# Token-major gates and branches, keys split around the mixer's output product, and PSUM as three pairs and two banks

## The chip, the cores and the metric

One core of one Trainium2 chip runs the whole program; the other cores are idle. The metric is the device time of one execution in microseconds. A core has TensorE (PE, with its weight loads listed as PEld), VectorE (DVE), ScalarE (ACT), GpSimd (POOL) and SyncE (SP, whose queue issues the weight DMAs). Each executes its own instructions in order and waits on semaphores for the others. PE writes its results to PSUM, whose eight banks of 128x512 float32 are read back by DVE and ACT.

## The reference

Two layers over 256 tokens of width 1024, in float32:

```python
for l in range(DEPTH):
    x = x + 0.5 * swiglu(rms_norm(x, ffn1_norm[l]), ffn1_w_gu[l], ffn1_w_down[l])
    h = rms_norm(x, mix_norm[l])
    z = h @ w_in[l]
    q_a, k_a, v_a, q_b, f_b, i_b, og_b, gate_a, gate_b = jnp.split(z, split_at, axis=-1)
    # rotary on q_a, k_a; dilated_attention over 3 groups x 4 heads; y_a (T, 1024):
    y_a = dilated_attention(q_a, k_a, v_a) @ w_att_branch[l]       # 512 -> 1024
    # gated linear recurrence over 8 heads, norm per head:
    o_b = rms_norm(hgrn2_recurrence(q_b, f_b, i_b, lb_all[l]), hgrn_head_norm[l])
    o_b = o_b * jax.nn.silu(og_b)
    y_b = o_b @ w_hgrn_branch[l]                                   # 1024 -> 1024
    merged = jax.nn.sigmoid(gate_a) * y_a + jax.nn.sigmoid(gate_b) * y_b
    x = x + merged @ w_mix_out[l]
    x = x + cross_attention(rms_norm(x, xattn_norm[l]), rms_norm(mem, mem_norm[l]), ...)
    x = x + 0.5 * swiglu(rms_norm(x, ffn2_norm[l]), ffn2_w_gu[l], ffn2_w_down[l])
return rms_norm(x, final_norm)
```

The output gate `og_b` and the two mixer gates are 1024 wide each. Cross-attention has 4 heads of 256 and takes its keys and values from 256 memory tokens, which do not depend on `x`.

## The kernel before, in words

**Products.** Every product is done in split form: a float32 operand is cast to a high part (fp32r) and the rest is kept as a low part, and three of the four partial products are summed. The weights stream from memory in chunks of 16 blocks of 128x128, in the order in which the program takes them. ACT casts half a chunk (8 blocks, called a half here) to its high part (`whi`, L104), DVE subtracts it for the low part (`wlo`, L110). High parts are made three halves ahead of use and low parts two (`prep`, called by `take`, L113). Five buffers hold high parts, four hold low parts.

There are two loops. The feature-major loop `fm` (L303) has the weight block stationary and the activation moving: one matmul of 512 columns (high and low part of the 256 tokens, L316) and one of 256 (L317) a block; its result has features on partitions and tokens along the row. ACT copies one half out of PSUM (L337) and DVE adds the other (L340). The token-major loop `tm` (L347) has 128 tokens of the activation stationary and four weight blocks moving (512 columns): three matmuls (L290 to L292) for each of two token tiles, six for four blocks. Its result has tokens on partitions and is complete in PSUM. Before the change `tm` is used for the values of both mixers (L809, L819) and of cross-attention.

**Order.** The program's order is written out by the code as it runs; nothing reorders it. At the first `take` of each half, `tick` (L179) runs deferred evacuations that are due and then one step of a side job: the recurrence `hgrn` (L610) and the attention heads (L712) are generators that yield between steps, and take turns. In most of the mixer a step is taken every second half (`pace`). `drain` (L760) runs what is left at the end of the mixer's input products. A norm runs the same way with precedence (`urgent_norm`, L405).

**PSUM.** One pool of four pairs (two banks each). `pair()` is what `fm` and `tm` accumulate in; `bank()` (L153) takes a whole pair and uses half of it. The recurrence's step that computes its output holds two (L674) until the norm's scale is applied to them in its next step (L693).

**The mixer.** `mixer` (L767) runs 8 feature-major products for the recurrence's forget gates and queries, then 12 for attention queries and keys (`query_key`), between them the values and the output gate (`out_gate`, L835: 4 feature-major products) and 3 of the 8 mixer gate products (`gate`, L869); 5 more gate products follow. The gates are multiplied by the norm's scale on DVE (L830), and ACT applies Silu (L838) and Sigmoid (L872) to whole tiles of 128x1024. The recurrence's output is transposed by PE to feature-major (L702), multiplied there by gain and output gate on DVE (L707) and split into high and low part. The branches (L890 to L901) are 8 feature-major products, each with 4 attention blocks and 8 recurrence blocks for one 128-wide column of the result; DVE multiplies by the gates (L896), adds (L898), and ACT and DVE split the sum. Then comes the output product `w_mix_out` (`mm_resid`, L903).

**Cross-attention.** `xattn` (L940) begins with four feature-major products for keys, then four for queries, whose heads' scores are side jobs; values are token-major; at the end four heads write one bank each (12 matmuls of 256 columns, L286 to L288), which ACT casts (L270) and DVE subtracts (L273).

## Time and profile before

| | |
|---|---|
| runs | 1644.33, 1646.98, 1646.46 us; median 1646.46 |
| profiled execution | 1643.66 us, of which the span is 1641.9 us |
| PE, PEld, DVE, ACT, POOL busy | 1624.8, 1415.7, 1236.6, 926.1, 65.6 us |
| mean granted PE clock | 0.998 |
| weights | 288.94 MB moved in all, mean 176 GB/s; a chunk of 1 MB lands in 4.8 us |
| layer 0: first feed-forward, mixer's input products, branches, output product, cross-attention, second feed-forward | to about 196 us, 477, 510, 534, 638, 822 |

The page's first part gives busy time of each engine; a busy engine may still wait inside an instruction, and PE's rows overlap. The chain of waits follows the end back to what released it. The answers by time list each instruction with its start, its duration, the engine, the line and the tiles, and in brackets how long the engine was idle just before and which instruction ended that. A view by stretch gives, between two times, the busy time of each engine and the number of instructions that touch the stretch. Rows "x6" are six like instructions in a row, with one duration from the first's start to the last's end.

### The profile page before, as it was taken

The numbers are of one execution on the slowest core, as the hardware profiler recorded it, in microseconds if no ns is written. First come the engines' busy times: TensorE is split into PE (matmuls) and PEld (weight loads), VectorE is DVE, ScalarE is ACT, GpSimd is POOL, SyncE is SP. The second block draws the span as 40 slices with busy tenths as digits, with TensorE's granted clock in tenths as the row PEclk, the third lists the DMA queues.
The fourth block names the chain that finished last, engine by engine and source line by source line (L and its number), as shares of the span: only waits on it lengthen the run. The fifth ranks groups of instructions, "written<-read, shape, count | busy, mean of one in ns | idle before, by whom it ended". The sixth has DMA issues, their size and how long they took to land.

```text
span 1641.9 us, 26458 instructions
## 1 busy us (share of the span) xinstructions
PE 1624.8 (99%) x10818; PEld 1415.7 (86%) x10818; DVE 1236.6 (75%) x1808; ACT 926.1 (56%) x1385; POOL 65.6 (4%) x46
## 2 busy tenths in 40 slices
PE   9999999999999999999999999999999999999998
PEld 7888888888888888888888888888888888888887
DVE  7887696767868868877677777967678788688764
ACT  6665445566655656655456555445565656466542
POOL 0000000111100000000000000010110000000000
PEclk9999999999999999999999999999999999999999
DMA  8455444444445534555455564444444445355552
GB/s 305 180 191 211 189 155 173 162 157 152 154 150 184 183 151 167 193 188 197 183 185 196 182 224 177 162 155 160 174 142 159 162 179 181 129 206 180 194 189 79
DMA packets 41593, 288.94 MB, mean 176 GB/s; under 512 B 4864, under 2 KB 4992, under 8 KB 7424
## 3 DMA queue, kind: packets, MB, share of 16 engines
q1 hardware_dynamic: 41040, 286.67, 48.7%
q8 instruction: 85, 1.39, 0.3%
q10 hardware_dynamic: 432, 0.59, 0.1%
q14 instruction: 36, 0.29, 0.1%
HBM read 286.18 MB, written 1.05 MB: 175 GB/s over the span
## 4 chain that ended last, share of the span: by engine, by line
PE 86%; DVE 9%; ACT 2%; issue 2%; POOL 0%; DMA 0%; POOLq 0%; ACTq 0%
PE pair L316 46%; PE pair L317 23%; DVE wlo L110 3%; PE pair L290 3%; PE pair L292 3%; PE pair L291 3%; DVE join L340 1%; PE pair L636 1%; DVE join L896 1%; PE pair L720 1%; PE pair L754 1%; PE pair L329 1%; DVE slot L273 0%; PE pair L288 0%; PE pair L287 0%
## 5 line engine op out<-in xcount | busy, mean ns | idle before, releaser
L316 PE MATMUL pair<-slot,whi 128*128 128x512 f32 x3808 | 1342.0, 396 | 2.8 <-DVE slot L273 2.5
L317 PE MATMUL pair<-slot,wlo 128*128 128x256 f32 x3808 | 1066.1, 280 | 0.0
L316 PEld LDWEIGHTS pair<-slot,whi 128*128 128x128 f32 x3808 | 713.7, 187 | 165.8 <-ACT whi L104 3.1
L317 PEld LDWEIGHTS pair<-slot,wlo 128*128 128x128 f32 x3808 | 719.2, 189 | 0.8
L110 DVE TENSOR_TENSOR wlo<-raw,whi 128x1024 fp32r<-128x1024 f32 x532 | 641.6, 1221 | 40.6 <-ACT whi L104 40.3
L104 ACT CAST whi<-raw 128x1024 fp32r<-128x1024 f32 x532 | 546.8, 1047 | 16.6 <-issue 8.5
L337 ACT COPY join<-pair 128x512 f32<-128x512 f32 x136 | 79.4, 585 | 181.9 <-PE pair L317 181.8
L340 DVE TENSOR_TENSOR join<-pair,join 128x512 f32<-128x512 f32 x136 | 93.7, 690 | 99.9 <-ACT join L337 99.7
L280 ACT ACTIVATE slot<-x,vecs 128x256 fp32r<-128x256 f32 x64 | 30.8, 505 | 134.0 <-DVE x L427 132.8
L290 PE MATMUL pair<-whi,slot 128*128 128x512 f32 x224 | 89.7, 401 | 0.0
L292 PE MATMUL pair<-whi,slot 128*128 128x512 f32 x224 | 87.5, 391 | 0.0
L291 PE MATMUL pair<-wlo,slot 128*128 128x512 f32 x224 | 87.4, 390 | 0.0
L427 DVE SCALAR_TENSOR_TENSOR x<-pair,x 128x256 f32<-128x256 f32 (+1 forms) x80 | 42.4, 530 | 50.3 <-PE pair L317 48.8
L270 ACT CAST slot<-join 128x256 fp32r<-128x256 f32 (+1 forms) x120 | 51.7, 435 | 50.2 <-DVE join L898 26.0
L337 ACT COPY slot<-pair 128x512 f32<-128x512 f32 x48 | 28.0, 583 | 68.6 <-PE pair L317 68.6
L504 ACT ACTIVATE tmp<-join 128x256 f32<-128x256 f32 x88 | 36.4, 418 | 53.2 <-DVE join L503 53.2
L503 DVE TENSOR_TENSOR join<-join,bc 128x512 f32<-128x512 f32 x88 | 60.5, 693 | 5.1 <-ACT bc L403 2.4
L340 DVE TENSOR_TENSOR slot<-pair,slot 128x512 f32<-128x512 f32 x48 | 33.0, 688 | 35.6 <-ACT slot L337 35.6
L856 POOL TENSOR_TENSOR join<-join,sinb 128x512 f32<-128x512 f32 x24 | 44.7, 1860 | 378.0 <-ACT join L855 366.2
L273 DVE TENSOR_TENSOR slot<-join,slot 128x256 fp32r<-128x256 f32 (+1 forms) x120 | 54.0, 455 | 2.8 <-ACT slot L270 2.8
L292 PEld LDWEIGHTS pair<-whi,slot 128*128 128x128 f32 x224 | 42.1, 188 | 9.2
L281 DVE SCALAR_TENSOR_TENSOR slot<-x,vecs,slot 128x256 fp32r<-128x256 f32 x64 | 29.6, 483 | 27.0 <-ACT slot L280 27.0
(184 smaller groups left out, 1027.7 us busy)
## 6 DMA issues: line engine op xcount, KB each, us to landing
raw<-w SPq DMA_DIRECT2D x266, 1024.0 KB, 4.8
slot<-mem SPq DMA_DIRECT2D x6, 512.0 KB, 6.6
raw<-w SPq DMA_DIRECT2D x3, 512.0 KB, 7.5
y<-slot SPq DMA_DIRECT2D x3, 256.0 KB, 2.3
cst<-cst SPq DMA_DIRECT2D x1, 721.0 KB, 10.2
x<-x SPq DMA_DIRECT2D x2, 256.0 KB, 4.2
x<-x SPq DMA_DIRECT2D x1, 512.0 KB, 6.8
raw<-w SPq DMA_DIRECT2D x1, 256.0 KB, 4.4
```

Source lines behind the costliest of these rows:

```text
L104: nc.scalar.copy(self.hi[i], r)
L110: nc.vector.tensor_tensor(self.lo[i], r, self.hi[i].bitcast(F32), op=OP.subtract)
L270: nc.scalar.copy(h, src)
L273: nc.vector.tensor_tensor(l, src, h.bitcast(F32), op=OP.subtract)
L290: nc.tensor.matmul(out, ah, wh, start=first, stop=False)
L291: nc.tensor.matmul(out, ah, wl, start=False, stop=False)
L292: nc.tensor.matmul(out, al, wh, start=False, stop=last)
L316: nc.tensor.matmul(whole[:, i * 512:(i + 1) * 512], wh, act.parts(k), start=k == 0, stop=False)
L317: nc.tensor.matmul(whole[:, i * 512:i * 512 + T], wl, act.hi(k), start=False, stop=k == K - 1)
L337: nc.scalar.copy(d, right)
L340: nc.vector.tensor_tensor(d, left, d, op=OP.add)
L503: nc.vector.tensor_tensor(two(t), two(t), both(n.bc), op=OP.mult)
```

## The change

1. PSUM becomes three pairs and a second pool of two single banks, which `bank()` now takes from. The recurrence's two output banks become one pair; the final norm's statistics take a pair.
2. The output gate and the mixer gates become token-major: 2 products of 512 columns instead of 4, and 4 instead of 8. ACT copies them out of PSUM with the norm's scale. The recurrence's output is multiplied by the output gate before it is transposed (one step more), and the gain goes into the split after it.
3. The branches become token-major, attention first and recurrence second, for two halves of 512 columns. DVE multiplies by the gates and adds; then PE turns the sum back to feature-major, four blocks of 128 columns in two banks, two calls of `tick` later, and ACT and DVE split it.
4. Half of the cross-attention keys (two of the four products) move ahead of the output product of the mixer.
5. The order of the input products is written anew. A side job steps at every half from the tenth query-key product on, as before.

```diff
-    psum = ent(tc.tile_pool(name="psum", bufs=4, space=bass.MemoryType.PSUM))
+    psum = ent(tc.tile_pool(name="psum", bufs=3, space=bass.MemoryType.PSUM))
+    psum1 = ent(tc.tile_pool(name="psum1", bufs=2, space=bass.MemoryType.PSUM))
...
     def bank():
-        return pair()[:, :512]
+        return psum1.tile([P, 512], F32, name="bank")
...
-    def tm(name, l, c, act, evac):
+    def tm(name, l, c, act, evac, K=KD):
...
-        bs = [bank(), bank()]
+        both_tiles = pair()
+        bs = [both_tiles[:, :512], both_tiles[:, 512:]]
...
         while ("og", l) not in flags:
             yield True
+        for i in range(2):
+            o = os_[:, 512 * i:512 * (i + 1)]
+            nc.vector.tensor_tensor(o, o, sog[i][:, hh * 512:(hh + 1) * 512], op=OP.mult)
+        yield
         for i in range(2):
             b = bank()
...
-            for h in range(2):
-                k = 4 * hh + 2 * i + h
-                o = tmp()
-                nc.vector.scalar_tensor_tensor(o, b[:, h * T:(h + 1) * T], vec("hgrn_head_norm", l, k),
-                                               sog(k), op0=OP.mult, op1=OP.mult)
-                out.put(k, o, later=1)
+            for f in (out.high_gain, out.low_gain):
+                for h in range(2):
+                    k = 4 * hh + 2 * i + h
+                    f(k, b[:, h * T:(h + 1) * T], vec("hgrn_head_norm", l, k))
...
+        def rows(c, col, d, func=None):
+
+            def evac(*bs):
+                for i, b in enumerate(bs):
+                    if c == 0:
+                        d[i] = slot()
+                    nc.scalar.activation(d[i][:, c * 512:(c + 1) * 512], b, AF.Copy, scale=n.r[:, i:i + 1])
+                if func and c == 1:
+                    func()
+            tm("w_in", l, col + c * 512, h, evac)
...
+        def gate(u):
+            def sigmoid():
+                for t in gates[0] + gates[1]:
+                    nc.scalar.activation(t, t, AF.Sigmoid)
+            g, c = divmod(u, 2)
+            rows(c, (CGA, CGB)[g], gates[g], sigmoid if g == 1 else None)
...
+        order = [(values_b, 2), (values_a, 3), (out_gate, 1), (None, 1), (out_gate, 1), (None, 2), (gate, 1), (None, 2),
+                 (gate, 3)]
...
+        def branch(c):
+            def attention_part(*bs):
+                m = [join(), join()]
+                for i, b in enumerate(bs):
+                    nc.vector.tensor_tensor(m[i], b, gates[0][i][:, c * 512:(c + 1) * 512], op=OP.mult)
+
+                def hgrn_part(*bs):
+                    for i, b in enumerate(bs):
+                        g = gates[1][i][:, c * 512:(c + 1) * 512]
+                        nc.vector.tensor_tensor(g, b, g, op=OP.mult)
+                        nc.vector.tensor_tensor(m[i], m[i], g, op=OP.add)
+                    defer(2, turn)
+
+                def turn():
+                    for k in (0, 2):
+                        b = bank()
+                        for kk in range(2):
+                            for i in range(2):
+                                nc.tensor.transpose(b[:, kk * T + i * P:kk * T + (i + 1) * P],
+                                                    m[i][:, (k + kk) * P:(k + kk + 1) * P], ident)
+                        mg.put(4 * c + k, b, n=2)
+                tm("w_hgrn_branch", l, c * 512, hout, hgrn_part)
+            tm("w_att_branch", l, c * 512, aout, attention_part, AH)
+        for c in range(2):
+            branch(c)
+        filler()
         r = nxt()
         mm_resid("w_mix_out", l, mg, KD, r)
...
-        operand(k, mn, "xattn_wkv", hm)
-        operand(q, n, "xattn_wq", h)
+        x_operand(l, k, mn, "xattn_wkv", hm, (4, 6))
+        x_operand(l, q, n, "xattn_wq", h, (0, 2, 4, 6), lambda hd: sides.append(head(hd)))
...
-        r = mixer(l, r, resid("xattn_norm", l, 1.0))
-        r = xattn(l, r, hm, resid("ffn2_norm", l, 1.0))
+        keys = Act()
+        r = mixer(l, r, resid("xattn_norm", l, 1.0),
+                  lambda: x_operand(l, keys, memn["n"], "xattn_wkv", hm, (0, 2)))
+        r = xattn(l, r, hm, keys, resid("ffn2_norm", l, 1.0))
```

How the instructions move, at two places of layer 0. The first is the end of the mixer's gates, on PE and on ACT. A name such as `slot_4622` is one tile; `pair_4758` and `bank_4638` receive the fourth head's attention output, `pair_4714` and `pair_4538` the last gate product. PE before:

```order
L317 MATMUL pair_4714<-slot_1634,wlo_4670 128x256
L754 MATMUL pair_4758<-slot_4723,slot_3133 128x256
L754 MATMUL pair_4758<-slot_4723,slot_3375 128x256
L754 MATMUL pair_4758<-slot_4723,slot_3544 128x256
L756 MATMUL pair_4758<-slot_4724,slot_3133 128x128
L756 MATMUL pair_4758<-slot_4724,slot_3375 128x128
L756 MATMUL pair_4758<-slot_4724,slot_3544 128x128
L316 MATMUL pair_4714<-slot_1765,whi_4668 128x512
```

and ACT before, where `slot_4622` is that output's high part and `slot_4712` the last gates' tile:

```order
L270 CAST slot_4622<-pair_4758 128x256
L337 COPY slot_4712<-pair_4714 128x512
L872 ACT_TABLE_LOAD
L872 ACTIVATE slot_4129<-slot_4129 128x1024
L872 ACTIVATE slot_4415<-slot_4415 128x1024
L872 ACTIVATE slot_4606<-slot_4606 128x1024
L872 ACTIVATE slot_4712<-slot_4712 128x1024
L104 CAST whi_4791<-raw_4641 128x1024
```

PE now (L299 is the last gate matmul, `pair_4647` the first branch product, `slot_3858` the first two heads' output, `slot_4550` the last two's):

```order
L299 MATMUL pair_4538<-whi_4539,slot_1903 128x512
L764 MATMUL bank_4638<-slot_4607,slot_3132 128x256
L764 MATMUL bank_4638<-slot_4607,slot_3374 128x256
L764 MATMUL bank_4638<-slot_4607,slot_3543 128x256
L766 MATMUL bank_4638<-slot_4608,slot_3132 128x128
L766 MATMUL bank_4638<-slot_4608,slot_3374 128x128
L766 MATMUL bank_4638<-slot_4608,slot_3543 128x128
L297 MATMUL pair_4647<-whi_4567,slot_3858 128x512
```

and ACT now:

```order
L844 ACTIVATE slot_4534<-pair_4538,rstd_2032 128x512
L844 ACTIVATE slot_4536<-pair_4538,rstd_2032 128x512
L859 ACT_TABLE_LOAD
L859 ACTIVATE slot_4203<-slot_4203 128x1024
L859 ACTIVATE slot_4205<-slot_4205 128x1024
L859 ACTIVATE slot_4534<-slot_4534 128x1024
L859 ACTIVATE slot_4536<-slot_4536 128x1024
L271 CAST slot_4550<-bank_4638 128x256
L104 CAST whi_4648<-raw_4513 128x1024
```

The fourth head's last step moved from inside the last gate product to behind it, and its cast on ACT from ahead of the sigmoids to behind them.

The second place is PE between the branches and the output product. Now the first product of keys (`pair_4887`) stands there, and eight transposes of the second half's sum (`join_4810`, `join_4811`) lie in its middle:

```order
L324 MATMUL pair_4887<-slot_1546,wlo_4851 128x256
L927 MATMUL bank_4914<-cst_92,join_4810 128x128
L927 MATMUL bank_4914<-cst_92,join_4811 128x128
L927 MATMUL bank_4914<-cst_92,join_4810 128x128
L927 MATMUL bank_4914<-cst_92,join_4811 128x128
L927 MATMUL bank_4922<-cst_92,join_4810 128x128
L927 MATMUL bank_4922<-cst_92,join_4811 128x128
L927 MATMUL bank_4922<-cst_92,join_4810 128x128
L927 MATMUL bank_4922<-cst_92,join_4811 128x128
L323 MATMUL pair_4887<-slot_1579,whi_4849 128x512
```

Before, the last branch product was followed at once by the output product; now 8 blocks of keys, these transposes and 24 more blocks of keys lie between.

More of the change, by code (lines that the diff above doesn't have):

```diff
@@ L938, in scores, with x_operand, evac, stage1 @@
         return pt
[L940 removed]
+    def x_operand(l, d, norm, name, act, js, then=None):
+        for j in js:
+            def evac(left, right, j=j):
+                t = join()
+                def stage1():
+                    nc.vector.tensor_tensor(two(t), two(t), both(norm.bc), op=OP.mult)
+                    d.put(j, t, later=1, n=2)
+                    if then:
+                        defer(2, lambda: then(j // 2))
+                add_halves(two(t), left, right, stage1)
+            fm([(name, l, (j + i) * P, act, KD) for i in range(2)], evac)
+    def xattn(l, res, hm, k, nxt):
         h, n = res.act, res.norm
```

85 lines of the change are left out of this document (28 added, 57 removed).

## The prediction

> **What bounds the kernel now.** I read the page's shares first, then the chain of waits, then the order of time on PE with the start of every matmul.
>
> ```profile
> span 1641.9 us, 26458 instructions
> PE 1624.8 (99%) x10818; PEld 1415.7 (86%) x10818; DVE 1236.6 (75%) x1808; ACT 926.1 (56%) x1385; POOL 65.6 (4%) x46
> PE 86%; DVE 9%; ACT 2%; issue 2%; POOL 0%; DMA 0%; POOLq 0%; ACTq 0%
> ```
>
> PE sets the end: it is busy for 99% of the span and carries 86% of the chain. So an edit is worth what it does to PE's own work, or to a gap in it. Work taken off DVE or ACT is worth nothing by itself. A matmul's "us" overlaps the next one's, so PE's price is the distance from start to start. The next view is PE's rows by stretch (two answers of it, the last row from the second), for the 512-column matmul of the feature-major loop (L316; one per weight block of 128x128, followed by one L317 of 256 columns), and for the first of each three in the token-major loop.
>
> ```profile
> core 0: us, PE busy (x) PEld busy (x), PEclk, DMA share, GB/s
> 456.99:467.59 10.60, 10.60 (x32) 5.63 (x31) 1.00 0.35 114
> 1266.51:1276.90 10.39, 10.39 (x31) 5.61 (x31) 1.00 0.32 114
> 477.20:514.30 37.10, 37.10 (x107) 19.73 (x106) 1.00 0.48 170
> 652.63:827.01 174.38, 174.38 (x505) 94.07 (x504) 1.00 0.52 188
> ...
> 292.77:299.60 6.83, 3.91 (x10) 1.88 (x10) 1.00 0.39 148
> ```
>
> Each stretch runs from one such matmul's start to another's; one or two counted rows only touch its edges. So the first two are 30 blocks each, the third 105, the fourth 503: 0.3533, 0.3463, 0.3533 and 0.3467 us a block. The feature-major loop has two paces, a slow one of 0.353 and a quick one of 0.347, at a granted clock of 1.00 in all four, and it keeps its pace until the next interruption. The first two rows are the same place in layer 0 and layer 1. The branches (third row) run at the slow pace throughout. The token-major loop made 30 matmuls in 6.83 us, 0.2277 each; six of them serve four blocks, so 0.3415 a block.
>
> **The change, part by part.** All sums are against the profiled execution (1643.66 us, span 1641.9); the median of the runs shown is 1646.46, and a difference carries over to it.
>
> *Gates and branches become token-major.* The streamed columns are the same (768 a block in both forms). Per layer 64 blocks of the output gate, 128 of the two mixer gates and 96 of the branches move. The branches gain 0.3533 - 0.3415 = 0.0118 on 192 blocks of both layers, 2.3 us. For the 384 gate blocks the gain lies between 0.0052 and 0.0118 each, 2.0 to 4.5 us; the first two rows say that layer 1 was quick where layer 0 was slow, so I take one slow block in four (0.0069) and 2.6 us. Together **-4.9**.
>
> The Trainium skill speaks against this term: "TensorE: Matmul & The Clock Gate", section "Back-to-back issue gap", gives a warm matmul N/2.4 + 2.5 ns. An estimate from it is 325 ns a block in the first form and 324 in the second, hence 0.7 us instead of 4.9. The rows above do not agree: they show 347 or 353 against 341.5, and I go by them.
>
> DVE loses the adds and the multiplications by the norm for the gates, and ACT keeps about as much; PE hides both, so that counts nothing.
>
> *The merged branches must be turned.* Four times in the program eight transposes come between matmuls. The trace has the same step at the recurrence's output:
>
> ```profile
> 408.36 0.28 PE L317 MATMUL pair<-slot,wlo 128*128 128x256 f32 x1
> 408.48 1.03 PE L702 MATMUL pair<-cst,slot 128*128 128x128 f32 x8
> 409.26 0.48 PE L316 MATMUL pair<-slot,whi 128*128 128x512 f32 x1
> 409.58 0.28 PE L317 MATMUL pair<-slot,wlo 128*128 128x256 f32 x1
> ...
> 412.13 1.08 PE L702 MATMUL pair<-cst,slot 128*128 128x128 f32 x8
> 413.36 0.47 PE L316 MATMUL pair<-slot,whi 128*128 128x512 f32 x1 [0.15 <-DVE tmp L707]
> ```
>
> The first step holds PE for 0.78 and the next matmul is 0.09 late (0.32 to its successor instead of 0.23): 0.87 us, **+3.5** for four. The turn also waits for DVE's last of four operations (0.69 us each by L340 in the groups below, 2.76 with no hand-over) while PE does 12 matmuls of 0.2277, 2.73: from 0 to 0.3 each, taken as **+0.4** in all.
>
> ```profile
> L110 DVE TENSOR_TENSOR wlo<-raw,whi 128x1024 fp32r<-128x1024 f32 x532 | 641.6, 1221 | 40.6 <-ACT whi L104 40.3
> L340 DVE TENSOR_TENSOR join<-pair,join 128x512 f32<-128x512 f32 x136 | 93.7, 690 | 99.9 <-ACT join L337 99.7
> ...
> L273 DVE TENSOR_TENSOR slot<-tmp,slot 128x256 fp32r<-128x256 f32 x16 | 5.7, 419 | 0.0
> ```
>
> *Gaps that go.* Two are in the rows below, the third in the rows above.
>
> ```profile
> 514.53 0.28 PE L317 MATMUL pair<-slot,wlo 128*128 128x256 f32 x1
> 516.06 0.47 PE L316 MATMUL pair<-slot,whi 128*128 128x512 f32 x1 [1.25 <-DVE slot L273]
> ...
> 382.98 0.83 PE L716 MATMUL pair<-slot 128*128 128x128 f32 x6
> 384.46 1.56 PE L720 MATMUL pair<-slot 128*128 128x256 f32 x6 [0.65 <-DVE slot L725]
> ```
>
> At 514.53 the output product waits for the last merged operand: 1.53 from start to start where 0.12 is normal, 1.41. Now 32 blocks of keys stand there, 11 us, and the operand is turned 8 blocks into them. At 382.98 six matmuls take 1.48 where they otherwise take 0.67 (419.65 - 418.99 is 0.66 at the next head, rows further down): the second tile of the scores had no free pair, since the recurrence held two; 0.81. With single banks apart it has one. At 412.13 the step takes 1.23 instead of 0.78, behind the same shortage: 0.45. Twice each: **-5.3**. Only the first is sure; the others could leave 2.5 us of that.
>
> *Waits that come.* First, ACT at the end of the gates. The last head's attention output is cast on ACT now behind the sigmoids, not ahead of them (the order shows it), and the branches begin with the product that needs it as its fourth operand.
>
> ```profile
> 300.06 0.39 PE L292 MATMUL pair<-whi,slot 128*128 128x512 f32 x1
> 300.28 0.39 PE L316 MATMUL pair<-slot,whi 128*128 128x512 f32 x1
> ...
> 300.48 1.27 ACT L823 ACTIVATE slot<-pair,rstd 128x512 f32<-128x512 f32 x2 [4.34 <-PE pair L292]
> 301.64 1.05 ACT L104 CAST whi<-raw 128x1024 fp32r<-128x1024 f32 x1
> ...
> 471.70 1.46 PE L754 MATMUL pair<-slot 128*128 128x256 f32 x6
> 473.00 0.83 PE L756 MATMUL pair<-slot 128*128 128x128 f32 x6
> 473.58 0.48 PE L316 MATMUL pair<-slot,whi 128*128 128x512 f32 x1
> ...
> 473.86 0.37 ACT L270 CAST slot<-pair 128x256 fp32r<-128x256 f32 x1 [2.17 <-PE pair L756]
> ...
> 477.29 1.28 ACT L872 ACT_TABLE_LOAD   x1
> 478.58 3.90 ACT L872 ACTIVATE slot<-slot 128x1024 f32<-128x1024 f32 x4
> 482.39 1.98 ACT L104 CAST whi<-raw 128x1024 fp32r<-128x1024 f32 x2
> ```
>
> Call T the moment PE leaves the gates. ACT starts its two copies at T + 0.20 (300.48 - 300.28), is free for the table load at T + 1.36, begins the sigmoids 1.29 later, is through 3.81 after that (482.39 - 478.58), T + 6.46, and has cast the operand at T + 6.83. PE does the head's last step (1.88, plus 0.09) and 18 matmuls (4.10) and wants it at T + 6.07. Wait: 0.8 a layer, **+1.6**. The weight casts queue behind the sigmoids too, but three halves of eight blocks (8.2 us of PE) are cast ahead. DVE's next low half follows the operand's (0.42 and 1.22, rows L273 and L110 above) and ends near T + 8.5, just when PE wants it. If that cover fails, it costs another 0.5 to 1 a layer; if the cast slips ahead, the whole wait is nothing.
>
> Beside the table load row the Trainium skill has "ScalarE: Activation LUTs", section "What ACT_TABLE_LOAD costs": about 1283 ns and a drain of about 1380. The trace shows the 1.28 and no drain (477.29 + 1.28 against 478.58). By the page this wait would be 2.2 a layer and the total 2.8 us more.
>
> Second, the four heads of cross-attention write one bank each, and of two banks the third head needs the first's back.
>
> ```profile
> 612.17 0.28 PE L286 MATMUL pair<-slot 128*128 128x256 f32 x1
> ...
> 612.40 1.28 DVE L273 TENSOR_TENSOR slot<-pair,slot 128x512 fp32r<-128x512 f32 x2
> ```
>
> PE began the third head at 612.17; DVE left the first head's bank at 612.40 + 0.69 = 613.09. Nothing in the change moves either, so PE waits 0.92 and a hand-over: **+1.9** for two layers. The fourth head then finds its bank free. No DMA is added, SP and POOL get nothing new, and the weights lie in memory in the new order.
>
> *Sum:* -4.9 + 3.5 + 0.4 - 5.3 + 1.6 + 1.9 = **-2.8 us**, so 1640.9 for a profiled execution and 1643.7 for the median. By the ends of the terms: -2.0 to -4.5 for the gates; -2.8 to -5.3 for the gaps; 0 to 5.5 for the waits; and 0.0066 a block either way for each stretch elsewhere that changes its pace, such as the 67 blocks of the output product in each layer (0.4 each).
>
> **The rivals.**
>
> *A, the waits do not come* (the cast and the bank are in time; for it: each is short, 0.8 and 0.9; against: both follow from rows that the change leaves in their order): -2.8 - 3.5 = -6.3, 1640.2.
>
> *B, no gain in pace.* The paces are states, not costs of a form: the slow one was entered after an interruption, and the token-major stretch is only 30 matmuls. If the new stretches cost what the old ones did: -2.8 + 4.9 = +2.1, 1648.6. For it: two paces in one loop; against: no token-major stretch quoted is slower than the quick pace. The page's rule on the issue gap, above, leads here, with 0.7 of gain left: 1647.9 by that estimate.
>
> *C, slower: DVE's lag holds the two banks.* At a head's scores DVE came late:
>
> ```profile
> 418.99 0.83 PE L716 MATMUL pair<-slot 128*128 128x128 f32 x6
> 419.65 1.46 PE L720 MATMUL pair<-slot 128*128 128x256 f32 x6
> ...
> 425.17 0.55 DVE L725 SCALAR_TENSOR_TENSOR slot<-pair,cst 128x384 f32<-128x384 f32 x1
> ```
>
> DVE reached the scores 5.5 us after PE had written the first of them (425.17 - 419.65). Four pairs hid that. Steps now come every half of weights (2.7 us) and two apart share a bank, so a bank must be free some 3.6 to 5.5 us after it is written (one half and one step, or two halves). A lag beyond that stops PE for the difference: with 1 us at six steps of each layer, -2.8 + 12 = +9.2, 1655.7. Against: DVE loses the gates' work exactly there. It decides from a lag of about 4 us on.
>
> **How the numbers follow.** A measurement of this kernel tells about 0.2%, 3.3 us, from no change. The forecast -2.8 has 0.60, with its own range 1641 to 1646.5; it lies so near the bound that I give 0.22 of it to faster and 0.38 to the same. A has 0.18 (faster). B has 0.12 (0.09 same, 0.03 slower). C has 0.10 (slower). Faster 0.40, same 0.47, slower 0.13. The range 1639.8 to 1649.0 takes in A and B and leaves C and the far ends out.
>
> **What would show it.** In the changed kernel's trace: gate and branch stretches near 0.2277 a matmul; four steps of eight transposes near 0.87 us; no gap ahead of the output product; a wait of about 0.8 us in the first branch product for ACT's cast behind the sigmoids; one of about 0.95 at the third cross-attention head for DVE. Gaps at the recurrence's or the heads' steps with a DVE reader of a bank as releaser would show C. Wrong altogether would be long feature-major stretches, such as 652 to 827 (503 blocks, 6.6 ns apart in the two paces, 3.3 us), changing their pace though the program there is the same.

## The result and the profile after

| | before | after |
|---|---|---|
| median of the runs (4 each, on one chip) | 1645.39 us | 1656.53 us |
| ratio after to before | | 1.0076, 95% interval 1.0062 to 1.0090 |
| span of the profiled execution | 1641.9 us | 1653.1 us |

The change made the kernel slower by 0.8%. The forecast of 1643.7 us (range 1639.8 to 1649.0, slower at 0.13) was wrong. First the page of the changed kernel: span and busy time.

```profile
span 1653.1 us, 25840 instructions
PE 1626.2 (98%) x10562; PEld 1406.0 (85%) x10562; DVE 1191.5 (72%) x1716; ACT 920.0 (56%) x1357; POOL 65.2 (4%) x46
```

DVE lost 45 us of work and POOL got none; PE has 256 instructions fewer and is busy 1.4 us longer, although nothing was added to it but 32 transposes. So PE waits more, and some of its work is slower. Both stand at one place of each layer. PE by time, inside the first product of the mixer gates in layer 0:

```profile
410.96 0.39 PE L299 MATMUL pair<-whi,slot 128*128 128x512 f32 x1
416.81 1.62 PE L726 MATMUL bank<-slot 128*128 128x128 f32 x6 [5.46 <-DVE slot L288]
418.22 2.50 PE L730 MATMUL pair<-slot 128*128 128x256 f32 x6
420.37 0.58 PE L297 MATMUL pair<-whi,slot 128*128 128x512 f32 x1
```

The second head's scores (L726) need a single bank. The recurrence's output was turned into that bank at 407.6, and DVE's low parts (L288) still read it. From 410.96 to 416.81 are 5.85 us where 0.23 is normal: a wait of 5.62, and the same at 1227.06 in layer 1. Then the twelve small matmuls take 3.56 us (416.81 to 420.37) where the step took 1.77 before the change (from 418.99 on). The view by stretch around this place tells why (PEclk is the granted clock):

```profile
core 0: us, PE busy (x) PEld busy (x) DVE busy (x) ACT busy (x) POOL busy (x), PEclk, DMA share, GB/s
407.34:411.35 4.01, 4.01 (x22) 3.08 (x20) 4.01 (x6) 2.33 (x4) 0.98 (x1) 1.00 0.01 2
411.35:416.81 5.46, 0.00 (x1) 0.03 (x1) 4.27 (x9) 3.30 (x6) 1.60 (x1) 0.70 0.54 192
416.81:420.50 3.69, 3.69 (x13) 3.25 (x13) 2.23 (x4) 0.00 (x0) 0.00 (x0) 0.52 0.23 40
420.50:424.50 4.00, 4.00 (x24) 3.37 (x23) 3.58 (x5) 1.22 (x3) 0.00 (x0) 1.00 0.54 229
```

After the idle stretch PE is granted 0.52 of its clock for 3.7 us, then 1.00 again. The Trainium skill, "TensorE: Matmul & The Clock Gate", section "Part 1: The HAM clock gate (the "warmup" mystery)", says that a window of about 3.4 us without work halves the clock and about 3.4 us of work bring it back. The 3.7 us at 0.52 agree with the second half of that. The first half doesn't hold so here: a mean of 0.70 over the idle 5.46 us means that the clock was at half for some 3.3 of them, so 2.1 us without work had been enough; the last section comes back to it. So the place costs 5.62 + 1.79 us in layer 0 and 5.62 + 1.63 in layer 1, 14.7 in all. The spans differ by 11.2: the rest of the program is 3.5 quicker. That is near the -2.8 that was forecast for all of it, in part by luck, as is shown further down.

Who is late? ACT and DVE by time, from the second output gate product's end on:

```profile
383.66 1.27 ACT L844 ACTIVATE slot<-pair,rstd 128x512 f32<-128x512 f32 x2 [4.34 <-PE pair L299]
384.94 1.28 ACT L852 ACT_TABLE_LOAD   x1
386.24 2.00 ACT L852 ACTIVATE slot<-slot 128x1024 f32<-128x1024 f32 x2
388.14 1.98 ACT L104 CAST whi<-raw 128x1024 fp32r<-128x1024 f32 x2
```

```profile
389.21 1.23 DVE L110 TENSOR_TENSOR wlo<-raw,whi 128x1024 fp32r<-128x1024 f32 x1 [7.22 <-ACT whi L104]
...
396.41 1.22 DVE L110 TENSOR_TENSOR wlo<-raw,whi 128x1024 fp32r<-128x1024 f32 x1 [0.26 <-ACT whi L104]
397.69 0.69 DVE L880 TENSOR_TENSOR slot<-slot,cosb 128x512 f32<-128x512 f32 x1
399.57 0.69 DVE L881 TENSOR_TENSOR slot<-slot,join 128x512 f32<-128x512 f32 x1 [1.20 <-POOL join L876]
400.18 1.22 DVE L110 TENSOR_TENSOR wlo<-raw,whi 128x1024 fp32r<-128x1024 f32 x1
401.32 0.68 DVE L347 TENSOR_TENSOR slot<-pair,slot 128x512 f32<-128x512 f32 x1
...
412.99 0.69 DVE L881 TENSOR_TENSOR slot<-slot,join 128x512 f32<-128x512 f32 x1 [1.16 <-POOL join L876]
...
415.79 1.65 DVE L288 SCALAR_TENSOR_TENSOR slot<-bank,vecs,slot 128x256 fp32r<-128x256 f32 x4
```

DVE reads the bank 8 us after PE has written it. Two things precede. DVE idled 7.22 us for a weight cast that stood on ACT behind the gate's copies and Silu. And the five rows from 396.41 on are DVE's round for one query-key product: 5.5 us (396.41 to 401.92, the next L110) of which 1.2 is a wait for POOL, while PE makes such a product in 5.6 (16 blocks of 0.347 or 0.353). The new order has three of them in a row (numbers 7 to 9 in the code, which counts from 0; 383.5 to 402.1, with the first head's scores between); DVE has no time there to catch up, or to do a side step. Which of the two matters, and whether the single banks do, the experiments must tell.

### The profile page after: what moved, and what is told of

It reads as the page before. It is cut to its first block, busy times and chain, and to the rows that moved or that the text cites. A ratio compares the mean times of both kernels' runs of the same rounds, so it can differ in the third digit from the quotient of the medians.

```text
span 1653.1 us, 25840 instructions
## 1 busy us (share of the span) xinstructions
PE 1626.2 (98%) x10562; PEld 1406.0 (85%) x10562; DVE 1191.5 (72%) x1716; ACT 920.0 (56%) x1357; POOL 65.2 (4%) x46
## 3 DMA queue, kind: packets, MB, share of 16 engines
HBM read 286.18 MB, written 1.05 MB: 174 GB/s over the span
## 4 chain that ended last, share of the span: by engine, by line
PE 89%; DVE 6%; ACT 3%; issue 1%; POOL 1%; DMA 0%; POOLq 0%; ACTq 0%; DVEq 0%
PE pair L323 41%; PE pair L324 21%; PE pair L297 7%; PE pair L299 7%; PE pair L298 7%; DVE wlo L110 2%; PE bank L643 1%; PE pair L730 1%; PE pair L336 1%; POOL join L876 1%; ACT whi L104 1%; DVE join L347 0%; PE bank L764 0%; PE pair L688 0%; PE bank L293 0%
## 5 line engine op out<-in xcount | busy, mean ns | idle before, releaser
L323 PE MATMUL pair<-slot,whi 128*128 128x512 f32 x3232 | 1136.3, 395 | 0.0
L324 PE MATMUL pair<-slot,wlo 128*128 128x256 f32 x3232 | 904.2, 280 | 0.0
L323 PEld LDWEIGHTS pair<-slot,whi 128*128 128x128 f32 x3232 | 605.5, 187 | 136.6
L110 DVE TENSOR_TENSOR wlo<-raw,whi 128x1024 fp32r<-128x1024 f32 x532 | 640.3, 1221 | 63.6 <-ACT whi L104 55.4
L324 PEld LDWEIGHTS pair<-slot,wlo 128*128 128x128 f32 x3232 | 610.2, 189 | 1.0
L297 PE MATMUL pair<-whi,slot 128*128 128x512 f32 x512 | 204.9, 400 | 1.5 <-ACT slot L271 1.5
L299 PE MATMUL pair<-whi,slot 128*128 128x512 f32 x512 | 200.1, 391 | 0.0
L298 PE MATMUL pair<-wlo,slot 128*128 128x512 f32 x512 | 199.6, 390 | 0.0
L344 ACT COPY join<-pair 128x512 f32<-128x512 f32 x120 | 70.3, 586 | 181.8 <-PE pair L324 181.6
L347 DVE TENSOR_TENSOR join<-pair,join 128x512 f32<-128x512 f32 x120 | 82.8, 691 | 95.3 <-ACT join L344 95.3
L297 PEld LDWEIGHTS pair<-whi,slot 128*128 128x128 f32 x512 | 96.2, 188 | 21.5 <-ACT slot L271 2.3
L299 PEld LDWEIGHTS pair<-whi,slot 128*128 128x128 f32 x512 | 96.1, 188 | 21.1 <-DVE slot L274 0.3
L298 PEld LDWEIGHTS pair<-wlo,slot 128*128 128x128 f32 x512 | 96.3, 188 | 18.3
L288 DVE SCALAR_TENSOR_TENSOR slot<-x,vecs,slot 128x256 fp32r<-128x256 f32 x64 | 29.6, 484 | 27.1 <-ACT slot L285 27.1
```

The source lines that it names most:

```text
L110: nc.vector.tensor_tensor(self.lo[i], r, self.hi[i].bitcast(F32), op=OP.subtract)
L297: nc.tensor.matmul(out, ah, wh, start=first, stop=False)
L298: nc.tensor.matmul(out, ah, wl, start=False, stop=False)
L299: nc.tensor.matmul(out, al, wh, start=False, stop=last)
L323: nc.tensor.matmul(whole[:, i * 512:(i + 1) * 512], wh, act.parts(k), start=k == 0, stop=False)
L324: nc.tensor.matmul(whole[:, i * 512:i * 512 + T], wl, act.hi(k), start=False, stop=k == K - 1)
```

## The experiments

Each is a variant of the changed kernel unless it says otherwise. Ratios are to the kernel before, on the same chip, with 95% intervals. Waits are PE's, beyond the normal distance of two matmuls.

**1. Four pairs again.**

```diff
-    psum = ent(tc.tile_pool(name="psum", bufs=3, space=bass.MemoryType.PSUM))
-    psum1 = ent(tc.tile_pool(name="psum1", bufs=2, space=bass.MemoryType.PSUM))
+    psum = ent(tc.tile_pool(name="psum", bufs=4, space=bass.MemoryType.PSUM))
...
-        return psum1.tile([P, 512], F32, name="bank")
+        return pair()[:, :512]
```

> The changed kernel with PSUM as before (four pairs, a bank is half a pair), all else as changed. Theory 1, two single banks hold PE: the wait of 5.62 us ahead of the attention scores of each layer goes, and with it the doubled matmuls behind it (about 1.9 us a layer); so does the wait of 0.96 at the third cross-attention head. That is 15.0 + 1.9 less; the shortage of pairs at the scores and at the recurrence's output (0.81 and 0.45 a layer before) may return, up to 2.5. So 1656.5 - 16.9 + 0 to 2.5: 1640 to 1642. Theory 2, DVE is late with the weights' low halves as well and stops PE by itself: a wait of 1 to 5 us at a matmul that needs a low half stands in the same place in each layer, and the time stays above 1645.

1654.31 us, ratio 1.0056 (1.0039 to 1.0073): neither of the two times expected. The wait at the third cross-attention head went, but the one in the gates only moved to the scores' second tile. PE by time:

```profile
413.76 0.83 PE L725 MATMUL pair<-slot 128*128 128x128 f32 x6
419.39 1.19 PE L729 MATMUL pair<-slot 128*128 128x256 f32 x2 [4.79 <-DVE slot L287]
```

With all PSUM in one pool PE still waits 4.96 us, for the same instruction of DVE (L287 here is L288 there). So the two single banks aren't the cause: DVE's lag holds PE up in both splits of the eight banks. It did not stop PE at a weight's low half.

**2. The turned output in a pair.**

```diff
+        turned = pair()
         for i in range(2):
-            b = bank()
+            b = turned[:, 512 * i:512 * (i + 1)]
```

> Only the two tiles into which the recurrence's output is turned are taken from a pair; the attention scores then find a single bank free. Theory 1, the banks: the 5.62 us and the doubled matmuls behind them go, 15 us in all. The second four heads' turn comes about 7 us after the first's and now needs one of three pairs, while the gate product, the scores and the first turn hold the three; DVE leaves the first turn's at about 417.4 in layer 0, so up to 2 us of wait a layer at that turn: 1641.5 to 1646. Theory 2, DVE stops PE by its low halves: a wait of 1 to 5 us at a weight matmul remains, over 1646.

1675.53 us, ratio 1.0188 (1.0172 to 1.0203), some 30 us beyond what was expected. PE by time:

```profile
408.17 0.60 PE L715 MATMUL pair<-cst,slot 128*128 128x128 f32 x4
417.29 1.11 PE L715 MATMUL pair<-cst,slot 128*128 128x128 f32 x4 [8.52 <-DVE slot L288]
```

Half of the turn runs, the other half waits for DVE's reading of the first: both halves are one tile, which PE gets back as a whole. The same follows at the second turn, 4.90. The run tells nothing of the banks, but once more that DVE reads the turn 8 us late.

**3. Silu later, and 4. no gate multiplication.**

```diff
-            rows(c, COG, sog, silu)
+            rows(c, COG, sog, lambda: defer(2, silu))
```

> Silu of the output gate is issued two halves of weights later, so that the casts of the high parts that stand behind it on ACT go first. Theory 3, the lag of DVE starts at Silu: behind the two copies, the table load and Silu the next cast ended at 389.18 in layer 0 and DVE idled 7.22 us for it; without that DVE is some 4 to 7 us ahead at the recurrence's output, the bank is free in time, and the 15 us go: about 1641.5. Theory 4, the lag is made at the place itself (the gate multiplications, rotary's waits for POOL of 1.2 us each, ACT's wait for DVE's add): the output of the recurrence waits for Silu and moves with it, and a wait of 3 us or more for a bank stands at one of the next steps: 1650 to 1660.

```diff
-        for i in range(2):
-            o = os_[:, 512 * i:512 * (i + 1)]
-            nc.vector.tensor_tensor(o, o, sog[i][:, hh * 512:(hh + 1) * 512], op=OP.mult)
         yield
```

> The multiplication of the recurrence's output by the output gate is left out (four DVE instructions of 0.69 us in each layer, 2.5 us; its step stays, empty). If DVE's backlog at the place makes the wait (theory 4, and every theory by which DVE's queue holds the bank), the 5.62 us shrink by about 2.5 to 3.1, below which no clock is lost either: 1656.5 - 2 x (2.5 + 1.9) = 1647.7, or less where ACT's wait for DVE's add shrinks as well. If the wait is ACT's or POOL's, it stays at 5 us or more: 1655 to 1657.

1652.31 us, ratio 1.0048 (1.0033 to 1.0063), and 1653.67 us, 1.0055 (1.0040 to 1.0070). PE by time in the one and in the other:

```profile
414.97 0.91 PE L726 MATMUL bank<-slot 128*128 128x128 f32 x6 [3.59 <-DVE slot L288]
```

```profile
415.11 0.91 PE L723 MATMUL bank<-slot 128*128 128x128 f32 x6 [3.41 <-DVE slot L288]
```

The waits are 3.75 and 3.57 instead of 5.62. Run 3 came out as theory 4 has it, run 4 between its two cases. Each takes a third away and neither is the cause alone; and with 3.4 us of idle time the clock is lost all the same. Moving Silu cut DVE's idle time from 7.22 to 3.90, 3.3 us, of which 1.9 was left at the bank.

**5. PSUM alone, in the kernel before.** The edit is the part of the change's diff that run 1 took back, with the recurrence's two banks and the final statistics in a pair each.

> The kernel before with only PSUM changed: three pairs and two single banks, the recurrence's output in one pair, the final statistics in a pair. If the split of PSUM costs much by itself: two turns of the recurrence's output follow each other by 3.6 us and each takes both banks, DVE leaves the first's at about 413.2 in layer 0, so about 1 us of wait a layer; the third cross-attention head waits 0.95 a layer; against it the waits of 0.81 and 0.45 for a pair go. Sum +1.4: about 1645.8, no change that can be told. If single banks alone made the wait of 5.62 us, it would stand here too, and the time would be 1655 or more.

1649.62 us, ratio 1.0033 (1.0021 to 1.0045), more than the 1645.8 expected. PE by time at the second turn, and where the recurrence computes its output:

```profile
414.56 0.63 PE L704 MATMUL bank<-cst,slot 128*128 128x128 f32 x4 [0.73 <-DVE tmp L709]
415.34 0.63 PE L704 MATMUL bank<-cst,slot 128*128 128x128 f32 x4 [0.16 <-DVE tmp L709]
```

```profile
285.65 0.49 PE L682 MATMUL pair<-slot 128*128 128x128 f32 x2 [0.69 <-ACT tt L686]
```

The waits at the turn (0.90 and 0.32) and at the third head (0.96) came as expected. The rest, 0.85 twice a layer, is this variant's own: it still squares each half as soon as it is written, so PE's second half waits for ACT in the shared tile; the changed kernel squares both at once, and has no such wait. There is no wait of 5 us: the split of PSUM by itself does not make it, as run 1 says from the other side.

**6. The gates between the query-key products**, and side steps at every half once eight of these are done.

```diff
-        order = [(values_b, 2), (values_a, 3), (out_gate, 1), (None, 1), (out_gate, 1), (None, 2), (gate, 1), (None, 2),
-                 (gate, 3)]
+        order = [(values_b, 2), (values_a, 3), (out_gate, 2), (None, 1), (gate, 1), (None, 1), (gate, 1), (None, 1),
+                 (gate, 2)]
...
-                if u < AH * NG and not (f is gate and done[gate] == 0):
+                if u < AH * NG:
...
-            if u >= 10:
+            if u >= 8:
```

> The changed kernel with other places for the gates: output gate, one query-key product, output gate, two, gate, two, gate, two, gate, gate; so never three query-key products in a row (as it is, the 7th to 9th stand together ahead of the first gate), and a side step at every half from the 8th of them on. Theory 5, bunched query-key products overload DVE: one takes PE 5.6 us, and DVE 5.7 for it (two low halves 2.4, the add 0.7, rotary 1.3 and a wait of 1.2 for POOL), so any side step in a row of three leaves DVE behind; spread out, DVE is in time and the 5.62 us with the slow matmuls behind them go: 1656.5 - 15.0 = 1641.5. Theory 4, the lag is made by the two turns and the scores themselves: a wait of 3 us or more a layer at one of these, 1650 or more.

1644.40 us, ratio 1.0007 (0.9998 to 1.0017): the 5.62 us and the slow clock are gone. PE by time shows what is left in layer 0:

```profile
393.09 0.50 PE L297 MATMUL pair<-whi,slot 128*128 128x512 f32 x1 [1.68 <-DVE slot L701]
...
483.03 0.50 PE L298 MATMUL pair<-wlo,slot 128*128 128x512 f32 x1 [0.39 <-DVE wlo L110]
```

A wait of 1.85 for a pair behind Silu (DVE idles 6.34 for a cast there), one of 0.55 for a low half behind the sigmoids, and the third head's: 1644.4 rather than 1641.5.

**7. Rotary's addition later.**

```diff
                     nc.vector.tensor_tensor(d, d, both(cb), op=OP.mult)
+                    defer(1, stage3)
+
+                def stage3():
                     nc.vector.tensor_tensor(d, d, r, op=OP.add)
```

> Rotary's last addition is issued one half of weights later, so that DVE does not stand waiting for POOL in front of it. Between 389 and 416 us of layer 0 DVE waits so three times (1.20, 1.19 and 1.16). If DVE's queue is what holds the bank, it is free 3.5 us earlier and the wait shrinks from 5.62 to about 2.1, without loss of clock: 1656.5 - 2 x (3.5 + 1.9) = 1645.7. If ACT holds it (its casts of the output stand behind rotary's copies), the wait stays above 4 us: 1653 or more.

1655.77 us, ratio 1.0069 (1.0054 to 1.0084), and 4.82 us of wait, now at the second turn. A miss, and DVE's and POOL's rows by time say why:

```profile
401.14 1.86 DVE L110 TENSOR_TENSOR wlo<-raw,whi 128x1024 fp32r<-128x1024 f32 x1 [0.38 <-ACT whi L104]
...
406.18 2.39 DVE L708 TENSOR_TENSOR slot<-slot 128x512 f32<-128x512 f32 x2
```

```profile
400.17 1.74 POOL L876 TENSOR_TENSOR join<-join,sinb 128x512 f32<-128x512 f32 x1 [21.79 <-ACT join L875]
405.68 1.74 POOL L876 TENSOR_TENSOR join<-join,sinb 128x512 f32<-128x512 f32 x1 [3.76 <-ACT join L875]
```

DVE no longer waits in front of the addition. But its next instruction, begun while POOL runs, ends as late as if it had begun at POOL's end: POOL ends at 401.91, and 1.22 (L110 elsewhere) later is 403.13, against 403.00 measured; POOL ends at 407.42, and 1.29 (two L708 elsewhere) later is 408.71, against 408.57. The idle time became busy time. The Trainium skill, "SBUF — State Buffer", section "SBUF: two separate sides", says that DVE and GpSimd share a pair of ports as an exclusive lock, which a DVE instruction with two SBUF inputs needs as well; these rows agree.

**8. The cast first, and two heads in pairs.**

```diff
-            rows(c, (CGA, CGB)[g], gates[g], sigmoid if g == 1 else None)
+            rows(c, (CGA, CGB)[g], gates[g])
...
         drain()
+        for t in gates[0] + gates[1]:
+            nc.scalar.activation(t, t, AF.Sigmoid)
...
-            b = bank()
+            b = bank() if hd < 2 else pair()[:, :512]
             for d in range(2):
```

> The sigmoids of the gates are issued behind the last head's step, so that the cast of its output goes first on ACT; the third and fourth cross-attention heads write into pairs. The wait for the bank in the gates is left as it is. The two predicted waits (0.91 in the first branch product, 0.96 at the third head) go and nothing else moves: 1656.5 - 2 x 1.87 = 1652.8. If the later sigmoids hold DVE's multiplication by the gates or the weight casts behind them, a wait of about 1 us takes their place and half of that gain is lost: 1654.6.

1653.72 us, ratio 1.0060 (1.0045 to 1.0075). Both waits are gone from the trace and none stands in their place; the 5.61 us in the gates stay.

**9. Runs 6 and 8 together.**

> The gates between the query-key products (1644.4 by itself), and besides the cast of the last head's output ahead of the sigmoids and the third and fourth cross-attention heads in pairs. In the former the two waits measured 0.55 and 0.96 a layer; both go: 1644.4 - 3.0 = 1641.4. If they hide other work of DVE or ACT that is late as well, less than half of it shows: 1643 or more.

1643.84 us, ratio 0.9997 (0.9987 to 1.0006). The third head's wait went. The 0.55 stayed: in this order it is a low half that is late, not the cast of the head's output.

**10. With Silu later as well** (the edits of runs 3, 6 and 8).

> As the run with the gates between, the cast first and the heads in pairs, and besides Silu two halves of weights later. With the gates between, one wait of 1.85 us a layer is left in the mixer, for a pair that DVE frees behind a weight cast that stands behind Silu on ACT (DVE idles 6.34 us there). If Silu makes that lag it goes: 1641.4 - 3.7 = 1637.7. If the later Silu puts off the first turn, a wait of the same size stands there instead: 1641 to 1642.

1641.02 us, ratio 0.9983 (0.9973 to 0.9992). The wait for the pair fell from 1.85 to 1.05 only.

**11. Steps slower, order as changed, and 12. the new order alone.**

```diff
-            if u >= 10:
+            if u >= 12:
```

> The changed kernel's own order, with a side step at every second half up to the last query-key product (one product of gates and two query-key products later than it is). The turn of the recurrence and the scores then come at least two halves after the first gate product, in which DVE has only 4.9 us of weight work in 11 and can catch up. Theory 5, the row of three query-key products leaves DVE behind and the steps come before it has recovered: the 5.62 us go, and the drain has two steps of a head more, uncovered, some 2 us a layer: 1656.5 - 15.0 + 4 = 1645.5. Theory 4, the turns and the scores themselves make the lag: a wait of 3 us or more stays: 1652 or more.

Run 12 has the first two edits of run 6 and keeps `u >= 10`.

> The gates between the query-key products, but the side steps at every half only from the 10th of these on, as in the changed kernel. The first turn, the second and a head's scores then stand 5 halves and 1 half apart, so the scores come 2.7 us after a turn that took both banks' other half, as in the changed kernel. Theory 5, the order by itself cures the lag: no wait above 2 us at these steps; the drain has two more steps, about 2 us a layer: 1644.4 + 4 = 1648.4, or less by the 1.85 if that goes. If instead the distance of the steps cured it, a wait of 3 us or more stands at the scores or the turn: 1652 or more.

1656.82 us, ratio 1.0076 (1.0059 to 1.0093), and 1662.57 us, 1.0113 (1.0098 to 1.0128). PE by time, run 11 and then run 12:

```profile
416.84 0.39 PE L324 MATMUL pair<-slot,wlo 128*128 128x256 f32 x1 [1.13 <-DVE wlo L110]
...
477.97 2.45 PE L764 MATMUL bank<-slot 128*128 128x256 f32 x5 [4.57 <-ACT slot L756]
```

```profile
427.15 0.91 PE L726 MATMUL bank<-slot 128*128 128x128 f32 x6 [1.76 <-DVE slot L288]
...
480.46 2.08 PE L764 MATMUL bank<-slot 128*128 128x256 f32 x4 [6.26 <-ACT slot L756]
```

In run 11 the wait for the bank is gone. DVE is late by itself now: PE stops for low halves of weights, 1.29 here and 0.55 some 6 us earlier. In run 12 the wait at the scores is 1.92 instead of 5.62, so a third of it stays with the new order alone. The waits at these steps came out as theory 5 has it, but both times miss its forecast, by 11 and 14 us, and lie where the other case had them, for another reason. In both the time is lost at the drain, where one head's two last steps follow each other without cover: 4.73 and 6.42 us, where 2 were expected, and behind them PE runs at half clock for another 3.3 to 4.3 us a layer. So run 6 needs both its parts: the order takes most of the lag away, and the earlier steps empty the drain.

**13 and 14. The order of work on ACT**, in the best version and by itself. Run 14 puts the copies of the gate products one half later, behind a weight cast, and Silu one more; run 13 has that in run 10's kernel, and the sigmoids of the second gate two halves after the first's.

```diff
-            tm("w_in", l, col + c * 512, h, evac)
+            tm("w_in", l, col + c * 512, h, lambda *bs: defer(1, lambda: evac(*bs)))
...
-            rows(c, COG, sog, silu)
+            rows(c, COG, sog, lambda: defer(1, silu))
```

> As the run with all four edits (1641.0), and besides: the copies of the gate products out of PSUM are issued one half later, behind a weight cast, and the sigmoids of the second gate two halves after those of the first. Two waits are left there: 1.05 a layer for a pair at the first gate product, 0.55 a layer for a weight half in the first branch product, both behind ACT's copies and table functions. If ACT's order makes them, both go: 1641.0 - 3.2 = 1637.8. If DVE is late there for other reasons, they stay: 1640.5 to 1641.5.

> The changed kernel, its order of products and steps as it is; only the copies of the gate products are issued one half later and Silu one more, so that two weight casts go ahead of them on ACT. Theory 3, ACT's queue (copies that wait 4.34 us for the end of the product, table load, Silu, ahead of a cast for which DVE idles 7.22 us) makes the lag: DVE gets its half some 5 us earlier and keeps that up to the turn, the wait falls from 5.62 to about 1 without loss of clock: 1656.5 - 2 x (4.6 + 1.6) = 1644. Theory 5, the row of three query-key products makes it: what DVE gains at Silu it does not keep, as when Silu alone was moved (3.3 us less idle, 1.9 less wait), and 3 to 4 us of wait stay: 1650 to 1653.

Run 13: 1637.85 us, ratio 0.9967 (0.9956 to 0.9979), faster than both kernels. Its page has a span of 1635.8 us:

```profile
span 1635.8 us, 25844 instructions
```

Both remaining waits are gone from the trace. Run 14: 1651.89 us, ratio 1.0049 (1.0033 to 1.0064). DVE and PE by time:

```profile
384.62 1.23 DVE L110 TENSOR_TENSOR wlo<-raw,whi 128x1024 fp32r<-128x1024 f32 x1 [1.51 <-PE pair L298]
388.26 0.56 DVE L735 SCALAR_TENSOR_TENSOR slot<-bank,cst 128x384 f32<-128x384 f32 x1 [2.41 <-PE bank L726]
...
414.56 1.66 DVE L288 SCALAR_TENSOR_TENSOR slot<-bank,vecs,slot 128x256 fp32r<-128x256 f32 x4
```

```profile
415.58 0.77 PE L726 MATMUL bank<-slot 128*128 128x128 f32 x2 [3.11 <-DVE slot L288]
```

Here DVE is level with PE at 388.26: it waits for the scores that PE is making. All of Silu's lag is gone, and yet 24 us later, at 412.47, PE begins to stand idle, and it waits 3.27 us for DVE at the bank. So most of the wait is made between the two, in the row of three query-key products with the side steps laid on it; ACT's order adds the other part (5.62 - 3.27).

## Why the prediction was wrong, step by step

**The step that failed** is the price and the weight of rival C. It named the mechanism (DVE late, PSUM not free, steps every half) and its total of 1655.7 lies within a microsecond of the 1656.5 measured, but that nearness is luck: it was priced as 1 us at six steps, and it got a tenth of the chances. The forecast itself put this wait at nothing. What came is one wait of 5.62 us in each layer and, behind it, 1.6 to 1.8 us of half clock, which appeared in no term.

The argument against C was "DVE loses the gates' work exactly there". DVE did lose it. But a sum of work says nothing on a queue that runs in order. Before, another product stood between any two query-key products, token-major or a gate's (DVE had about 3.8 us for the 5.6 of PE there: two low halves, an add, a multiplication); now the gates are fewer and longer, and between two of them three query-key products follow each other, each 5.5 us of DVE for 5.6 of PE. The prediction took from the new order only what it does to PE and to the end of the gates. Runs 6, 11, 12 and 14 show this cause, and runs 3 and 14 that ACT's order (Silu and the copies ahead of a weight cast) adds a part, about 2 of the 5.6 us; run 1 shows that C's other half, that the two banks are what is short, was wrong.

**Gates and branches, -4.9: right.** The row below is a stretch of the new branches: from one L297's start to another's, 19 groups of three matmuls in 12.97 us, 0.2275 a matmul where 0.2277 was taken.

```profile
484.83:497.80 12.97, 7.42 (x20) 1.00 0.66 241
```

**Turns, +3.5 and +0.4: right.** The four steps of eight transposes took 1.01, 0.93, 1.01 and 0.93 us, and the matmul behind each came 0.09 late: 4.2 in all, with DVE's hand-over inside the first of each layer. **Gaps, -5.3: right.** None of the three is in the trace.

**The wait for the cast, +1.6, and for the bank, +1.9: right.** PE by time:

```profile
484.04 0.50 PE L297 MATMUL pair<-whi,slot 128*128 128x512 f32 x1 [0.75 <-ACT slot L271]
```

```profile
616.61 0.39 PE L293 MATMUL bank<-slot 128*128 128x256 f32 x1 [0.80 <-DVE slot L274]
```

0.91 and 0.96 us a layer beyond the normal distance, where 0.8 and 0.95 were worked out; rival A, that they would not come, fell. With every wait taken out, run 13 has a span 6.1 below that of before, and A's sum, the forecast without waits, was -6.3.

**What would make it wrong** was put as a change of pace in long feature-major stretches; the stretch that was named there, 652 to 827, kept its 0.3467 (it runs from 655 to 831 now), but another changed, and helped. In layer 0's first feed-forward, where the program is the same in all kernels, a stretch of 60 us holds these matmuls, before and after:

```profile
130.00:190.00 60.00, 60.00 (x171) 1.00 0.56 207
```

```profile
130.00:190.00 60.00, 60.00 (x174) 1.00 0.59 211
```

Of the sixteen profiled kernels thirteen ran it at 0.3533 us a block and three (the changed one, runs 10 and 14) at 0.3467: 1.7 us on the 262 blocks from 109 to 201 us that no edit explains. So of the 3.5 us that the rest of the program gained, some 1.9 (the lead of the changed kernel's trace where the mixer begins) are not the change's, and 1.6 are. The terms as measured add up to -4.9 + 4.2 - 5.3 + 1.8 + 1.9 = -2.3; the output product, which ran at 0.348 (layer 0) and 0.347 (layer 1) a block before and runs at 0.353 now, takes back some 0.8 of that (66 blocks a layer).

## What to carry to other kernels

Where engines run in order, compare their work stage by stage and in the order in which it is issued, not as sums: an engine at 72% of the span can be late by 8 us in a row of products that each fill it. When products of a lighter kind are made larger and fewer, ask what they had been spaced between. Each wait on PE of more than 3 us cost more than its length here, by an estimated 1.5 to 3.1 us (half of the time that PE then ran at half clock); waits of under 2 us did not, so two small waits may be cheaper than one long one.

## What the runs showed of the hardware

The granted clock changes on a fixed grid of time. In every profile the stretches at half clock that begin between 15 and 1620 us last 3.41 us or two or three times that, and their starts lie a whole number of 3.413 us apart, whatever PE does in between (run 14: 415.41 and 1227.79, 238 times). In the rows below the time is cut along this grid (columns as in the view by stretch above): layer 1 of run 14, layer 1 of the changed kernel, and layer 0 of run 3.

```profile
1224.37:1227.78 3.41, 1.45 (x7) 0.87 (x5) 2.64 (x5) 2.37 (x5) 0.70 (x1) 1.00 0.75 300
1227.78:1231.20 3.42, 2.28 (x9) 2.13 (x10) 3.38 (x7) 0.00 (x0) 0.00 (x0) 0.50 0.00 0
1231.20:1234.61 3.41, 3.41 (x10) 2.67 (x9) 1.47 (x3) 0.00 (x0) 0.00 (x0) 0.50 0.76 276
```

```profile
1225.87:1229.28 3.41, 1.58 (x7) 0.96 (x6) 2.25 (x4) 3.38 (x6) 2.59 (x1) 1.00 0.22 38
1229.28:1232.69 3.41, 0.00 (x0) 0.00 (x0) 3.37 (x8) 1.47 (x3) 0.00 (x0) 1.00 0.64 269
```

```profile
412.90:416.31 3.41, 1.34 (x9) 1.32 (x10) 3.41 (x6) 0.00 (x0) 0.00 (x0) 1.00 0.20 82
416.31:419.72 3.41, 3.41 (x9) 2.69 (x9) 2.69 (x5) 0.00 (x0) 0.00 (x0) 0.50 0.45 166
```

What decides in these profiles is how much of one such window PE stands idle. In run 14 it was idle for 1.96 of 3.41 us, and the next window ran at half clock; in the changed kernel it was idle for 1.83, and the next window, though all idle, still had the full clock. In run 3 PE had already run for 1.34 us at full clock after its wait when the clock was halved. Counted like this over all sixteen profiles, between 15 and 1620 us, each of the 22 changes to half clock followed a window with 1.96 us of idle time or more, and no window with 1.83 or less was followed by one. A window at half clock was followed by another when PE was idle in it for 0.65 us or more (1.14 in the second row), and by full clock at 0.44 or less.

So the price of a wait depends on where the grid cuts it. The 3.11 us of idle time in run 14 were followed by 3.25 us at half clock in layer 0 and by 5.7 in layer 1; idle times of 1.76 (run 12) and 1.68 us (run 6) lost no clock. The Trainium skill, "TensorE: Matmul & The Clock Gate", section "Part 1: The HAM clock gate (the "warmup" mystery)", has a window of about 3.4 us that runs freely. The starts agree with that. The Trainium skill has the clock halved after an idle window; here somewhat more than half of one was enough.

That DVE's instructions with two SBUF inputs stand still while POOL multiplies (run 7) was not expected either; it is why moving the addition alone did not win the 1.2 us at each of the 24 query-key products. Not settled is what sets the pace of the feature-major loop, 0.3467 or 0.3533 us a block: the granted clock is 1.00 in both, and it differs between executions in which nothing ahead of the stretch was edited.
